# A streaming-encoder trunk: one order of products for each pass, and a longer leash for VectorE

## The chip, the cores and the metric

One core of a Trainium2 chip. The metric is the time of one execution on the device, in microseconds (us). Engines are called as in the profile: PE is TensorE's matmul, PEld its weight load, DVE is VectorE, ACT ScalarE, POOL GpSimd, SP SyncE.

## What is computed

Two pre-norm residual layers over a sequence of 1024 frames and 1024 channels. Each layer projects the normalised input once, runs four token mixers on it, gates and merges them, and projects back:

```python
h = _rmsnorm(x, norm_w)
p = h @ w_in                               # 1024 x (all widths of the four mixers and the gates)
u_a = _rwkv7_branch(...); u_b = _retention_branch(...)
u_c = _ssd_branch(...);   u_d = _gdn_branch(...)
gates = jax.nn.sigmoid(gate_logits.reshape(b, s, N_BRANCH, D_MODEL))
merged = gates[:, :, 0] * (u_a @ w_branch[0]) + ... + gates[:, :, 3] * (u_d @ w_branch[3])
return x + merged @ w_out
```

RWKV-7 and gated DeltaNet (GDN) are recurrences; in chunks they need the inverse of a triangular matrix. A last RMSNorm follows the two layers. All in float32.

## The kernel before, in words

A *pass* is one layer (l) on one half of the frames (512): pass p = 2 l + half, four passes. The weights are cut into *slabs* of 128x512. Each is split into a high and a low part in fp32r (wh, wl), as is the activation (hH, hL), and a product is hH·wh + hL·wh + hH·wl: for one slab 8 matmuls with wh and 4 with wl (`slab_gemm`), into one of three PSUM banks named g. ACT or DVE makes wh (a cast), DVE makes wl by a subtraction in `low`, up to three slabs ahead of use; in the second pass of a layer both come back from DRAM, where SP kept them (ws). SP loads slabs five ahead into three raw buffers (`prefetch`).

A pass is a list of *items*, each with its products. `in.u.role` is an input of unit u: its result goes to one of a few SBUF places (PLACES: in0 to in3 have two, in4 and in5 one), and the item has to wait until a place is free (`unit_input`). `sm` and `lora` are small shared inputs, `merge.kind.i` the gate and the branch projection of a mixer that is through, `gate.i` and `proj.i` those of the last mixer, `norm` the start of the next pass's normalisation, `out.i` a slab of the output projection. The list was written by hand: FIRST for the first pass, PLAN for the other three; in PLAN the `out` items are those of the pass before.

Twelve *units* (UNITS: 2 retention, 4 GDN, 2 SSD, 4 RWKV heads or groups) do the mixers. A unit is a generator (`ret_front`, `gdn_front`, `gdn_mid` with `inverse`, `gdn_back` and so on) that writes a few instructions for all engines at each step and stops where PE would have to wait for another engine. At most two fronts are held at once; backs follow in order.

Nothing is scheduled on the chip: each engine runs its instructions in the order in which Python writes them. `mixers` weaves them. A planner's clock (`Clock`) adds up estimated times for each engine while instructions are written. At each turn `step(LEAD)` looks for a unit step whose inputs are ready by that clock at PE's time; if the clock of DVE is more than LEAD = 3 us beyond PE's, no unit step is written. Where no step is due, the next four or so matmuls of the next item are written (`products`). An item that cannot start yields None; then only unit steps follow until it can, whatever the lag (`step(1e9)`). In this text the product stream *stands* from the first such None to the next matmul of an item.

For the change of a pass: `norm` issues six loads of x on SP and starts `norm_steps`, which writes for each of 8 blocks one multiplication on DVE (`norm_block`), a cast to hH on ACT and a subtraction to hL on DVE (`norm_low`). hH and hL have one buffer each, so they are written after the last gate product of the pass. Until all blocks are written, h counts as not ready (`h_gemm`). Only in the first pass a few items can run early, on rows that are not normalised yet (rH, rL, in the buffers u), with the factor multiplied in afterwards. `proj.i` ends in three DVE instructions with an ACT copy between (`ev` in `proj`). All engine calls but matmuls have line 400 in the profile, matmuls 480, transposes 484.

Of the kernel before, what the change touches and what calls it, by code (L numbers as in the profile page):

```python
# [50 lines left out]
FIRST = items("""
sm in.0.k in.0.q in.0.v in.0.z0 in.0.z1 in.1.k in.1.q in.1.v in.1.z0 in.1.z1 in.2.v in.2.k in.2.q in.2.z in.3.v
in.3.k in.3.q lora in.3.z in.4.v in.4.k in.4.q merge.ret.0 merge.ret.1 merge.ret.2 merge.ret.3 merge.ret.4 in.4.z
in.5.v in.5.k in.5.q merge.ret.5 in.5.z in.6.x0 in.6.B in.6.C in.6.x1 merge.ret.6 merge.ret.7 in.6.z in.7.x0
in.7.B in.7.C in.7.x1 merge.gdn.0 merge.gdn.1 merge.gdn.2 in.7.z in.8.v in.8.k in.8.r in.8.z in.9.v in.9.k in.9.r
in.9.z merge.gdn.3 merge.gdn.4 in.10.v in.10.k in.10.r merge.gdn.5 merge.gdn.6 merge.gdn.7 merge.ssd.0 in.10.z
merge.ssd.1 in.11.v in.11.k in.11.r merge.ssd.2 merge.ssd.3 merge.ssd.4 in.11.z merge.ssd.5 merge.ssd.6
merge.ssd.7 gate.0 gate.1 gate.2 gate.3 gate.4 gate.5 gate.6 gate.7 norm proj.0 proj.1 proj.2 proj.3 proj.4 proj.5  # L60
proj.6 proj.7
""")

PLAN = items("""
in.0.k in.0.q in.0.v in.0.z0 in.0.z1 in.1.k in.1.q in.1.v in.1.z0 out.0 sm out.1 out.2 out.3 out.4 out.5 in.1.z1
in.2.v in.2.k in.2.q in.2.z in.3.v in.3.k in.3.q in.3.z in.4.v in.4.k in.4.q out.6 out.7 lora merge.ret.0
merge.ret.1 merge.ret.2 merge.ret.3 in.4.z in.5.v in.5.k in.5.q merge.ret.4 in.5.z in.6.x0 in.6.B in.6.C in.6.x1
merge.ret.5 merge.ret.6 merge.ret.7 in.6.z in.7.x0 in.7.B in.7.C in.7.x1 merge.gdn.0 merge.gdn.1 in.7.z in.8.v
in.8.k in.8.r in.8.z in.9.v in.9.k in.9.r in.9.z merge.gdn.2 merge.gdn.3 in.10.v in.10.k in.10.r merge.gdn.4
merge.gdn.5 merge.gdn.6 merge.gdn.7 merge.ssd.0 in.10.z merge.ssd.1 in.11.v in.11.k in.11.r merge.ssd.2  # L70
merge.ssd.3 merge.ssd.4 in.11.z merge.ssd.5 merge.ssd.6 merge.ssd.7 gate.0 gate.1 gate.2 gate.3 gate.4 gate.5
gate.6 gate.7 norm proj.0 proj.1 proj.2 proj.3 proj.4 proj.5 proj.6 proj.7
""")
# [38 lines left out]


SLABS = [sl for it in PLAN for sl in slabs_of(it)]
NSLAB = len(SLABS)
SLAB_AT = {sl: n for n, sl in enumerate(SLABS)}


def sequence(npass):

    seq = [(p - (it[0] == "out"), it) for p in range(npass) for it in (PLAN if p else FIRST)]
    return [x for x in seq if x != (npass - 1, ("norm",))] + [(npass - 1, it) for it in PLAN if it[0] == "out"]

# [147 lines left out]
class Clock:  # L271
# [89 lines left out]
    def ported(self, eng, name, ins):  # L361


        if eng == "scalar" or not ins or any(self.slot.get(x.tensor.name, ("",))[0] in ("m", "g", "y") for x in ins):
            return False
        return eng == "gpsimd" or name in ("tensor_tensor", "scalar_tensor_tensor", "tensor_copy", "copy") \
            or (name == "tensor_scalar" and int(np.prod(ins[0].shape[1:])) >= 32)

    def free(self, eng, port=False):
        return max(self.t[eng], self.port) if port else self.t[eng]  # L370
# [2 lines left out]
class Engine:  # L373
# [5 lines left out]
    def __getattr__(self, what):  # L379
        fn = getattr(self.real, what)  # L380

        def call(*a, **k):
            ops = [x for x in list(a) + list(k.values()) if hasattr(x, "ap") and hasattr(x, "tensor")]
            out = k.get("out", a[0] if a else None)
            outs = [out] + ([k["accum_out"]] if k.get("accum_out") is not None else [])
            n = max(int(np.prod(x.shape[1:])) for x in ops)
            if what == "dma_start":
                self.clock.transfer(self.name, a[0], a[1], int(np.prod(a[0].shape)) / 256)
            else:
                nm = "pow" if ALU.pow in a else what  # L390
# [9 lines left out]
            return fn(*a, **k)  # L400
        return call
# [21 lines left out]


class Trunk:
    LEAD = 3.0

    def __init__(self, ctx, tc, io, depth=DEPTH, dbg=None):
        self.tc, self.io, self.depth = tc, io, depth
# [39 lines left out]


    def mm(self, out, lhsT, rhs, **k):
        n, m = (int(np.prod(ap.shape[1:])) for ap in (rhs, lhsT))
        if rhs.dtype != F32:
            cost = max(n, 128) * 0.456e-3
        elif m <= 64:
            cost = 0.03 if m <= 32 else 0.11 if n <= 64 else n * 1.7e-3
        else:
            cost = 2 * max(n, m) * 0.85e-3
        self.ck.op("pe", [out], [lhsT, rhs], cost)
        self.nc.tensor.matmul(out, lhsT, rhs, **k)  # L480
# [6 lines left out]
    def setup(self):  # L487
# [793 lines left out]
    def mixers(self):  # L1281
# [815 lines left out]
```

## Time and profile before

| | us |
|---|---|
| median of 3 runs | 3675.07 |
| lowest and highest | 3674.42, 3675.59 |
| the profiled execution | 3677.53 |
| its span | 3675.8 |
| PE busy in it | 3535.3 |
| DVE, ACT, POOL busy | 2296.0, 1178.1, 572.1 |

The page gives busy time by engine, the granted clock of PE, the chain that ended last and groups of instructions with the idle time before each; "<-" in a row of waits names what ended the wait. A row of a stretch gives start and end in us, its length, then busy us of PE, PEld, DVE, ACT and POOL with counts, the clock granted (1.00 is full), the share of DMA and GB/s. A stretch's length less its PE busy time is called its idle time.

### The profile page before, as it was taken

To read this page: it belongs to the slowest core of one execution; us is meant where nothing else is said; L and a number is where in the kernel's file an instruction comes from. 1 tells how busy PE (TensorE), PEld (TensorE's weight loads), DVE (VectorE), ACT (ScalarE), POOL (GpSimd) and SP (SyncE) were. 2 spreads that over 40 slices of the span, in tenths; PEclk is the share of its full clock that TensorE was granted. 3 is DMA by queue.
4 is the path that set the end of the run, shared out by engine and by line. 5 is a ranking of instruction groups with operands and counts; after the bars stand their busy time and mean duration, and the time that the engine had idled before them with its cause. 6 is when DMAs were issued, how large, how long until landed. Compare 5 with 4: busy or idle time off the path is not lost.

```text
span 3675.8 us, 66687 instructions
## 1 busy us (share of the span) xinstructions
PE 3535.3 (96%) x24904; PEld 2855.0 (78%) x24904; DVE 2296.0 (62%) x6038; ACT 1178.1 (32%) x2714; POOL 572.1 (16%) x905
## 2 busy tenths in 40 slices
PE   8998999999999999999999989999999999999998
PEld 6776887777787888777777777877778788877777
DVE  5676767677356655466547676667764666564653
ACT  4333344333132223232224333433331322232221
POOL 2101012221110111122110101122211011112220
PEclk9998999999999999999999999999999999999999
DMA  6573565656665545444676556655566544544356
GB/s 236 174 232 130 196 211 190 200 165 208 210 211 160 150 133 146 134 111 128 199 252 226 185 187 200 208 185 172 185 215 225 177 152 144 149 132 132 104 153 214
DMA packets 359171, 654.21 MB, mean 178 GB/s; under 512 B 39872, under 2 KB 43328, under 8 KB 358848
## 3 DMA queue, kind: packets, MB, share of 16 engines
q1 hardware_dynamic: 347184, 629.92, 54.3%
q10 hardware_dynamic: 11664, 20.02, 1.6%
q8 instruction: 197, 3.23, 0.4%
q14 instruction: 126, 1.03, 0.1%
HBM read 400.23 MB, written 249.56 MB: 177 GB/s over the span
## 4 chain that ended last, share of the span: by engine, by line
PE 83%; DVE 10%; DMA 2%; ACT 2%; issue 1%; POOL 1%; SPq 0%; DVEq 0%; ACTq 0%; POOLq 0%
PE g L480 60%; PE m L480 17%; PE m L484 3%; PE y L480 3%; DVE invw L400 2%; DVE w L400 1%; DMA ws<-wh 1%; DVE wl L400 1%; DVE in L400 1%; DVE cvy L400 1%; DVE yB L400 1%; POOL rs L400 1%; DVE hL L400 0%; ACT w L400 0%; DVE GD L400 0%
## 5 line engine op out<-in xcount | busy, mean ns | idle before, releaser
L480 PE MATMUL g<-hH,wh 128*128 128x512 f32 x2600 | 1075.8, 414 | 0.0
L480 PE MATMUL g<-hL,wh 128*128 128x512 f32 x2600 | 1034.8, 398 | 16.0 <-DVE hL L400 15.9
L480 PE MATMUL g<-hH,wl 128*128 128x512 f32 x2576 | 745.7, 406 | 0.0
L480 PEld LDWEIGHTS g<-hL,wh 128*128 128x128 f32 x2600 | 492.3, 189 | 128.4 <-DVE hL L400 19.3
L480 PEld LDWEIGHTS g<-hH,wh 128*128 128x128 f32 x2600 | 492.0, 189 | 117.5 <-issue 7.1
L480 PEld LDWEIGHTS g<-hH,wl 128*128 128x128 f32 x2576 | 475.7, 190 | 112.1 <-issue 8.1
L480 PE MATMUL g<-u,wh 128*128 128x512 f32 (+1 forms) x1328 | 409.0, 412 | 18.8 <-DVE u L400 11.8
L400 DVE TENSOR_TENSOR wl<-raw,wh 128x512 fp32r<-128x512 f32 x456 | 331.1, 731 | 61.3 <-ACT wh L400 40.3
L400 ACT CAST wh<-raw 128x512 fp32r<-128x512 f32 x447 | 275.2, 619 | 252.5 <-DMA ws<-wh 106.8
L480 PEld LDWEIGHTS g<-u,wh 128*128 128x128 f32 (+1 forms) x1328 | 245.0, 190 | 81.5 <-DVE u L400 18.0
L400 POOL TENSOR_TENSOR rs<-rs,mhalf 128x4 f32<-128x4 f32 (+2 forms) x80 | 106.1, 1327 | 1011.3 <-DVE rs L400 980.4
L400 DVE SCALAR_TENSOR_TENSOR cvy<-cvraw,par,cvy 128x512 f32<-128x512 f32 x244 | 186.5, 764 | 76.8 <-ACT cvy L400 68.3
L480 PE MATMUL g<-u,wl 128*128 128x512 f32 x784 | 223.4, 403 | 0.0
L400 ACT COPY cvraw<-g 128x512 f32<-128x512 f32 (+1 forms) x160 | 93.5, 584 | 301.5 <-PE g L480 254.3
L480 PEld LDWEIGHTS g<-u,wl 128*128 128x128 f32 x784 | 146.3, 190 | 33.3 <-issue 0.5
L400 ACT ACTIVATE tg<-g 128x512 f32<-128x512 f32 x100 | 59.6, 596 | 267.0 <-PE g L480 258.8
L480 PE MATMUL g<-wh,hL 128*128 128x256 f32 x512 | 126.7, 285 | 6.9 <-DVE hL L400 6.9
L480 PE MATMUL g<-wh,hH 128*128 128x256 f32 x512 | 128.4, 288 | 0.0
L400 POOL TENSOR_SCALAR_AFFINE_SELECT GA<-GA 128x512 f32<-128x512 f32 x128 | 86.5, 681 | 249.8 <-ACT GA L400 215.6
L400 POOL TENSOR_TENSOR acc<-acc,tg 128x512 f32<-128x512 f32 x64 | 84.3, 1317 | 241.9 <-DVE tg L400 176.5
L400 ACT ACTIVATE in<-g 128x512 f32<-128x512 f32 x84 | 49.3, 596 | 187.5 <-PE g L480 182.0
L480 PE MATMUL m<-w,w 64*128 64x256 f32 (+1 forms) x640 | 108.3, 299 | 1.0 <-ACT w L400 1.0
(337 smaller groups left out, 5592.8 us busy)
## 6 DMA issues: line engine op xcount, KB each, us to landing
raw<-W SPq DMA_DIRECT2D x456, 256.0 KB, 3.3
ws<-wh SPq DMA_DIRECT2D x456, 256.0 KB, 3.5
ws<-wl SPq DMA_DIRECT2D x456, 256.0 KB, 3.8
wh<-ws SPq DMA_DIRECT2D x456, 256.0 KB, 2.6
wl<-ws SPq DMA_DIRECT2D x456, 256.0 KB, 3.0
w<-x ACTq DMA_DIRECT2D x32, 256.0 KB, 4.2
tg<-rope SPq DMA_DIRECT2D x16, 256.0 KB, 4.3
cvy<-rope SPq DMA_DIRECT2D x16, 256.0 KB, 4.3
```

The source lines that it names most:

```text
L400: return fn(*a, **k)
L480: self.nc.tensor.matmul(out, lhsT, rhs, **k)
L484: self.nc.tensor.transpose(out, in_, ident)
```

## The change

PLAN and FIRST are replaced by five lists, PLANS: one for each pass, and a last one with the eight `out` items of the last pass. They have the same items in another order. LEAD is 20 instead of 3. The list that numbers the slabs' places in DRAM is now PLANS[1]. `np.prod` in the planner becomes `math.prod`.

```diff
-FIRST = items("""
-sm in.0.k in.0.q in.0.v in.0.z0 in.0.z1 in.1.k in.1.q in.1.v in.1.z0 in.1.z1 in.2.v in.2.k in.2.q in.2.z in.3.v
...
-PLAN = items("""
-in.0.k in.0.q in.0.v in.0.z0 in.0.z1 in.1.k in.1.q in.1.v in.1.z0 out.0 sm out.1 out.2 out.3 out.4 out.5 in.1.z1
...
+PLANS = [items(text) for text in ("""
+in.0.k sm in.0.v in.0.q in.0.z0 in.0.z1 in.1.k in.1.q in.1.v in.2.v in.1.z0 in.2.k in.2.q in.3.v in.3.k lora in.3.q
...
+""", """
+out.0 out.1 out.2 out.3 out.4 out.5 out.6 out.7
+""")]
...
-SLABS = [sl for it in PLAN for sl in slabs_of(it)]
+SLABS = [sl for it in PLANS[1] for sl in slabs_of(it)]
...
-    seq = [(p - (it[0] == "out"), it) for p in range(npass) for it in (PLAN if p else FIRST)]
-    return [x for x in seq if x != (npass - 1, ("norm",))] + [(npass - 1, it) for it in PLAN if it[0] == "out"]
+    return [(p - (it[0] == "out"), it) for p in range(npass + 1) for it in PLANS[p] if (p, it) != (npass - 1, ("norm",))]
...
-    LEAD = 3.0
+    LEAD = 20.0
```

With the new lists the product stream stands 10 times in the whole program, with 104 DVE instructions written meanwhile; with the old ones 27 times, with 404. What that looks like on PE in pass 2, at the third GDN unit's inverse (its 32x32 matmuls, tiles invw and GE) and the second's chain (stgdn is its state, y its output, b its new values). Before, from the end of a stand to its middle:

```order
L484 MATMUL m_22338<-con_81,in_31_20921 128x128 x4
L480 MATMUL m_22365<-GA_19_20982,GR_18_20983 128x128
L480 MATMUL m_22365<-stgdn_1_100,GA_19_20982 128x128
L480 MATMUL y_21934<-stgdn_1_100,GA_19_20982 128x128
L480 MATMUL m_22372<-invw_14_22108,GE_27_22057 32x32 x16
L480 MATMUL m_22391<-b_71_22368,GA_19_20982 128x128
L480 MATMUL y_21934<-b_71_22368,GD_18_20984 128x128
L480 MATMUL m_22395<-invw_14_22108 32x32 x16
L480 MATMUL m_22414<-GA_19_20982,GR_18_20983 128x128
```

After, the same unit on PE (the products are tiles g; lines are 15 further down):

```order
L495 MATMUL g_22148<-hH_19118,wl_22058 128x512 x4
L495 MATMUL g_22148<-hH_19118,wh_22076 128x512
L495 MATMUL g_22148<-hL_19119,wh_22076 128x512
L495 MATMUL g_22148<-hH_19118,wh_22076 128x512
L495 MATMUL g_22148<-hL_19119,wh_22076 128x512
L495 MATMUL m_22183<-invw_14_21985,GE_27_21949 32x32 x16
L495 MATMUL m_22202<-b_71_22129,GA_19_21034 128x128
L495 MATMUL y_21930<-b_71_22129,GD_18_21036 128x128
L495 MATMUL g_22148<-hH_19118,wh_22076 128x512
L495 MATMUL g_22148<-hL_19119,wh_22076 128x512
```

Before, the inverse's first 32x32 matmuls follow the chain's stgdn matmuls at once, and no g product stands among these rows; after, 20 products of 128x512 stand between the stgdn matmuls and these, and more follow.

The second place is DVE at the end of pass 0. w are the loaded blocks of x, hL the low part of the normalised rows, and three rows on in/acc tiles and u are the evacuation of one proj item. Before:

```order
L400 SCALAR_TENSOR_TENSOR in_13_9680<-in_13_9680,g_10014 128x512
L400 TENSOR_TENSOR in_13_9680<-acc_1_2031,in_13_9680 128x512
L400 TENSOR_TENSOR acc_2_10013<-in_13_9680,u_4_9825 128x512
L400 SCALAR_TENSOR_TENSOR w_21_9814<-w_21_9814,par_67,w_17_9792 128x512
L400 TENSOR_TENSOR hL_9808<-w_24_9805,hH_9807 128x512
L400 SCALAR_TENSOR_TENSOR w_25_9820<-w_25_9820,par_67,w_17_9792 128x512
L400 TENSOR_TENSOR hL_9808<-w_21_9814,hH_9807 128x512
L400 TENSOR_TENSOR hL_9808<-w_25_9820,hH_9807 128x512
```

After, from the fourth proj item's evacuation on:

```order
L415 SCALAR_TENSOR_TENSOR in_5_9453<-in_5_9453,g_9916 128x512
L415 TENSOR_TENSOR in_5_9453<-acc_2_2176,in_5_9453 128x512
L415 TENSOR_TENSOR acc_3_9915<-in_5_9453,u_4_9753 128x512
L415 TENSOR_TENSOR hL_9850<-w_25_9877,hH_9849 128x512
L415 TENSOR_TENSOR wl_9962<-raw_9884,wh_9951 128x512
L415 SCALAR_TENSOR_TENSOR in_5_9572<-in_5_9572,g_9947 128x512
```

Before, the last hL row stands behind the evacuation of proj.7; after, behind that of proj.3, with those of proj.4 to proj.7 still to come.

The third place is PE in the first pass, around the input v of unit 0 (128x256 products). Before:

```order
L480 MATMUL m_369<-con_81,yC_272 128x16 x4
L480 MATMUL g_407<-wh_254,hH_274 128x256
L480 MATMUL g_407<-wh_254,hL_275 128x256
L480 MATMUL g_407<-wh_254,hH_274 128x256
L480 MATMUL g_407<-wh_254,hL_275 128x256
```

After:

```order
L495 MATMUL g_228<-u_1_107,wh_173 48x512
L495 MATMUL g_228<-u_1_108,wh_173 48x512
L495 MATMUL g_301<-wh_200,u_1_107 128x256
L495 MATMUL g_301<-wh_200,u_1_108 128x256
L495 MATMUL g_302<-wh_200,u_1_107 128x256
```

Before, these products read the normalised rows hH and hL; after, they read the rows that are not normalised (u_1_107, u_1_108) and follow the 48x512 products of `sm`.

At the end of pass 1, `norm` stands behind gate.7 in both; before, proj.0 to proj.7 follow it, after, proj.7 alone. At the end of pass 0, proj.0 and gate.7 stand before `norm`; at the end of pass 2 the list is as before.

More of the change, by code (lines that the diff above doesn't have):

```diff
@@ L49, in items @@
     return [tuple(int(x) if x.isdigit() else x for x in it.split(".")) for it in text.split()]
-FIRST = items("""
-sm in.0.k in.0.q in.0.v in.0.z0 in.0.z1 in.1.k in.1.q in.1.v in.1.z0 in.1.z1 in.2.v in.2.k in.2.q in.2.z in.3.v
-in.3.k in.3.q lora in.3.z in.4.v in.4.k in.4.q merge.ret.0 merge.ret.1 merge.ret.2 merge.ret.3 merge.ret.4 in.4.z
-in.5.v in.5.k in.5.q merge.ret.5 in.5.z in.6.x0 in.6.B in.6.C in.6.x1 merge.ret.6 merge.ret.7 in.6.z in.7.x0
-in.7.B in.7.C in.7.x1 merge.gdn.0 merge.gdn.1 merge.gdn.2 in.7.z in.8.v in.8.k in.8.r in.8.z in.9.v in.9.k in.9.r
@@ L58 @@
[L58 to L62, printed above, removed]
-PLAN = items("""
-in.0.k in.0.q in.0.v in.0.z0 in.0.z1 in.1.k in.1.q in.1.v in.1.z0 out.0 sm out.1 out.2 out.3 out.4 out.5 in.1.z1
-in.2.v in.2.k in.2.q in.2.z in.3.v in.3.k in.3.q in.3.z in.4.v in.4.k in.4.q out.6 out.7 lora merge.ret.0
@@ L67 @@
[L67 to L71, printed above, removed]
@@ L72 @@
-gate.6 gate.7 norm proj.0 proj.1 proj.2 proj.3 proj.4 proj.5 proj.6 proj.7
-""")
+PLANS = [items(text) for text in ("""
+in.0.k sm in.0.v in.0.q in.0.z0 in.0.z1 in.1.k in.1.q in.1.v in.2.v in.1.z0 in.2.k in.2.q in.3.v in.3.k lora in.3.q
+in.2.z in.1.z1 in.4.k in.3.z in.4.v merge.ret.0 merge.ret.1 in.5.k in.4.q in.5.v merge.ret.2 merge.ret.3 merge.ret.4
+in.4.z in.5.q in.6.x0 merge.ret.5 in.5.z merge.ret.6 in.6.B in.6.C in.6.x1 merge.ret.7 in.7.B in.7.x0 in.6.z in.7.x1
+merge.gdn.0 merge.gdn.1 merge.gdn.2 in.7.C in.8.v in.7.z in.8.k in.8.r in.9.v in.8.z in.9.k merge.gdn.3 in.9.r
@@ new lines @@
+in.9.z merge.gdn.4 merge.gdn.5 merge.gdn.6 merge.gdn.7 in.10.k in.10.r merge.ssd.0 in.10.v in.10.z merge.ssd.1
+in.11.v in.11.k in.11.r merge.ssd.2 merge.ssd.3 merge.ssd.4 in.11.z merge.ssd.5 merge.ssd.6 merge.ssd.7 gate.0
+gate.1 gate.2 gate.3 gate.4 gate.5 gate.6 proj.0 gate.7 norm proj.1 proj.2 proj.3 proj.4 proj.5 proj.6 proj.7
+""", """
+in.0.k in.0.z0 in.0.q out.0 in.0.v in.0.z1 in.1.k in.1.q in.1.v sm out.1 out.2 out.3 out.4 out.5 in.2.v in.1.z0
+in.2.q in.3.v in.2.k in.3.k in.3.q in.2.z out.6 in.1.z1 out.7 in.4.q in.4.k in.4.v lora merge.ret.0 in.3.z
@@ new lines @@
+merge.ret.1 merge.ret.2 in.4.z merge.ret.3 in.5.q in.5.k in.5.v in.5.z in.6.x0 merge.ret.4 in.6.B in.6.C in.6.z
+in.6.x1 merge.ret.5 merge.ret.6 merge.ret.7 in.7.C merge.gdn.0 in.7.x0 in.7.B in.7.x1 merge.gdn.1 in.7.z in.8.v
+in.8.k in.8.z merge.gdn.2 in.9.k in.8.r merge.gdn.3 merge.gdn.4 merge.gdn.5 merge.gdn.6 in.9.v in.9.r in.10.r
+merge.gdn.7 merge.ssd.0 in.9.z in.10.v in.10.k merge.ssd.1 in.11.v in.11.k in.10.z merge.ssd.2 merge.ssd.3 in.11.r
+merge.ssd.4 merge.ssd.5 merge.ssd.6 in.11.z merge.ssd.7 gate.0 gate.1 gate.2 gate.3 gate.4 gate.5 proj.0 gate.6
@@ new lines @@
+proj.1 proj.2 proj.3 proj.4 proj.5 proj.6 gate.7 norm proj.7
+""", """
+in.0.k sm in.0.z0 in.0.q in.0.v in.0.z1 in.1.k in.1.q in.1.v out.0 out.1 out.2 in.2.q out.3 in.2.v in.2.k in.3.v
+in.3.k out.4 in.1.z1 in.1.z0 in.2.z out.5 in.3.q in.3.z in.4.v in.4.k out.6 out.7 lora merge.ret.0 in.4.q
+merge.ret.1 merge.ret.2 merge.ret.3 in.5.q in.4.z in.5.v in.5.k merge.ret.4 in.6.C in.6.B merge.ret.5 in.5.z in.6.x1
+in.6.x0 in.7.B merge.ret.6 merge.ret.7 in.6.z in.7.x0 merge.gdn.0 merge.gdn.1 in.7.x1 in.7.C in.7.z in.8.v in.8.k
@@ new lines @@
+in.8.r merge.gdn.2 in.9.r in.8.z merge.gdn.3 in.9.v in.9.z in.9.k in.10.v in.10.k in.10.r merge.gdn.4 merge.gdn.5
+merge.gdn.6 merge.gdn.7 merge.ssd.0 in.10.z merge.ssd.1 in.11.v in.11.k in.11.r merge.ssd.2 merge.ssd.3 merge.ssd.4
+merge.ssd.5 merge.ssd.6 merge.ssd.7 in.11.z gate.0 gate.1 gate.2 gate.3 gate.4 gate.5 gate.6 gate.7 norm proj.0
+proj.1 proj.2 proj.3 proj.4 proj.5 proj.6 proj.7
+""", """
+in.0.q in.0.z1 in.0.k in.0.v in.0.z0 in.1.q in.1.k in.1.z0 out.0 sm out.1 in.1.v out.2 out.3 in.2.k out.4 out.5
@@ new lines @@
+in.1.z1 in.2.q in.2.v out.6 out.7 in.3.k in.3.q in.2.z in.3.v lora in.3.z merge.ret.0 merge.ret.1 in.4.v merge.ret.2
+in.4.k in.4.q merge.ret.3 in.5.k in.5.q in.4.z in.6.C in.5.v in.6.x0 in.6.B merge.ret.4 in.6.x1 merge.ret.5
+merge.ret.6 in.5.z in.6.z merge.ret.7 in.7.x0 merge.gdn.0 merge.gdn.1 in.7.C in.8.k in.7.x1 in.7.B in.7.z in.8.z
+in.8.v in.8.r in.9.v in.9.k merge.gdn.2 merge.gdn.3 in.9.z in.9.r in.10.v in.10.k in.10.r merge.gdn.4 merge.gdn.5
+merge.gdn.6 merge.gdn.7 merge.ssd.0 in.10.z in.11.v merge.ssd.1 in.11.r merge.ssd.2 merge.ssd.3 merge.ssd.4 in.11.k
@@ L76, in block_cols @@
+in.11.z merge.ssd.5 merge.ssd.6 merge.ssd.7 gate.0 gate.1 gate.2 gate.3 gate.4 gate.5 gate.6 gate.7 norm proj.0
+proj.1 proj.2 proj.3 proj.4 proj.5 proj.6 proj.7
+""", """
+out.0 out.1 out.2 out.3 out.4 out.5 out.6 out.7
+""")]
 def block_cols(kind, idx, role):
@@ L366, in ported @@
         return eng == "gpsimd" or name in ("tensor_tensor", "scalar_tensor_tensor", "tensor_copy", "copy") \
-            or (name == "tensor_scalar" and int(np.prod(ins[0].shape[1:])) >= 32)
+            or (name == "tensor_scalar" and int(math.prod(ins[0].shape[1:])) >= 32)
     def free(self, eng, port=False):
@@ L385, in call @@
             outs = [out] + ([k["accum_out"]] if k.get("accum_out") is not None else [])
-            n = max(int(np.prod(x.shape[1:])) for x in ops)
+            n = max(int(math.prod(x.shape[1:])) for x in ops)
             if what == "dma_start":
-                self.clock.transfer(self.name, a[0], a[1], int(np.prod(a[0].shape)) / 256)
+                self.clock.transfer(self.name, a[0], a[1], int(math.prod(a[0].shape)) / 256)
             else:
@@ L471, in mm @@
     def mm(self, out, lhsT, rhs, **k):
-        n, m = (int(np.prod(ap.shape[1:])) for ap in (rhs, lhsT))
+        n, m = (int(math.prod(ap.shape[1:])) for ap in (rhs, lhsT))
         if rhs.dtype != F32:
```

## The prediction, made before the run

> **What bounds the kernel now.** I read the head of the page first, then the row of cores, then the waits of PE, then stretches of the span by engine, and last the order of time inside the worst stretch.
>
> ```profile
> span 3675.8 us, 66687 instructions
> PE 3535.3 (96%) x24904; PEld 2855.0 (78%) x24904; DVE 2296.0 (62%) x6038; ACT 1178.1 (32%) x2714; POOL 572.1 (16%) x905
> core 0: 3675.8 us, clock 0.981
> ```
>
> PE is the bound: it idles for 3675.8 − 3535.3 = 140.5 us. The second loss is in the clock. A mean grant of 0.981 is (1 − 0.981) × 3675.8 = 69.8 us of full-speed time not granted. A new order removes no product, so only these two sums can shrink.
>
> The rows of PE's waits name VectorE nearly every time:
>
> ```profile
> PE g L480 <- DVE hL L400: 22.8, 6, 7.2
> PE m L484 <- DVE yB L400: 18.8, 9, 4.5
> PE m L480 <- DVE invw L400: 18.7, 19, 4.3
> PE m L480 <- DVE GR L400: 18.2, 5, 6.1
> ```
>
> VectorE is only 62% busy, so the waits are places where PE has been handed nothing but the dependent links of a unit's chain. The kernel's code says when that happens: the next product in PLAN cannot start (its `in` place is taken, or h is not ready), and only unit steps are written until it can. I followed the program in the order in which it is written and marked where the product stream stands. Before, it stands 27 times, and 404 VectorE instructions are written meanwhile. The thirteen stretches of the span that lie on unit inputs (us; length, then PE busy, PEld, DVE, ACT, POOL, then the granted clock):
>
> ```profile
> 103.60:131.00 27.40, 18.76 (x72) 13.19 (x71) 15.26 (x40) 4.87 (x12) 4.18 (x2) 0.77 0.18 63
> 277.50:293.30 15.80, 10.59 (x73) 9.18 (x72) 8.54 (x24) 3.04 (x7) 1.01 (x1) 0.87 0.10 35
> 329.50:354.00 24.50, 14.06 (x146) 11.71 (x145) 16.99 (x62) 3.04 (x8) 2.34 (x6) 0.58 0.17 53
> 403.70:419.20 15.50, 12.85 (x174) 11.30 (x173) 10.82 (x29) 3.03 (x6) 2.71 (x6) 0.89 0.35 105
> ...
> 588.70:597.00 8.30, 5.79 (x90) 5.06 (x90) 6.51 (x27) 2.78 (x7) 3.06 (x5) 0.79 0.54 186
> ...
> 2076.70:2097.10 20.40, 14.76 (x189) 12.85 (x189) 12.45 (x35) 4.23 (x10) 2.15 (x5) 0.86 0.25 86
> 2132.60:2156.00 23.40, 12.02 (x145) 10.02 (x144) 17.01 (x62) 3.04 (x8) 2.34 (x6) 0.71 0.17 57
> ...
> 2289.20:2303.00 13.80, 9.32 (x46) 7.74 (x44) 7.76 (x16) 4.08 (x13) 4.42 (x5) 0.75 0.15 53
> 2392.60:2399.00 6.40, 3.88 (x88) 3.40 (x88) 5.51 (x23) 2.77 (x7) 1.47 (x2) 1.00 0.49 157
> ...
> sum 168.40, PE 111.74 PEld 92.35 DVE 112.34 ACT 37.03 POOL 24.93; mean PE 8.60 PEld 7.10 DVE 8.64 ACT 2.85 POOL 1.92
> ```
>
> They hold 168.40 − 111.74 = 56.7 us of the idle time, and the sum of (1 − clock) × length over the rows with a clock below 1 is 6.3 + 2.1 + 10.3 + 1.7 + 1.7 + 2.9 + 6.8 + 3.5 = 35.2 us, half of the clock's loss. Within the stretch from 2132.6 the rows of PE in order of time show the chain alone:
>
> ```profile
> 2133.44 0.39 PE L480 MATMUL m<-GA,GR 128*128 128x128 f32 x2
> 2136.98 0.49 PE L480 MATMUL m<-stgdn,GA 128*128 128x128 f32 x2 [3.15 <-DVE stgdn L400]
> 2137.31 0.39 PE L480 MATMUL y<-stgdn,GA 128*128 128x128 f32 x2
> 2141.99 0.65 PE L480 MATMUL m<-invw,GE 32*32 32x32 f32 x32 [4.30 <-DVE invw L400]
> ```
>
> The other known losses lie at the first inverse of a pass (190.6, 1104.9, 1993.0, 2916.4), at the first normalisation (37.7) and at the three changes of pass (893, 1804.5, 2704), in the same columns:
>
> ```profile
> 37.70:57.00 19.30, 12.37 (x84) 11.73 (x84) 17.97 (x40) 7.05 (x14) 4.90 (x4) 0.82 0.42 140
> 190.60:207.00 16.40, 10.29 (x44) 7.67 (x43) 13.13 (x40) 5.93 (x11) 0.00 (x0) 0.80 0.58 190
> 893.00:938.00 45.00, 35.65 (x140) 27.39 (x139) 31.28 (x49) 15.06 (x26) 1.68 (x2) 0.92 0.65 219
> 1104.90:1116.00 11.10, 7.76 (x34) 5.72 (x33) 8.66 (x33) 2.41 (x6) 0.00 (x0) 0.85 0.32 94
> 1804.50:1822.00 17.50, 10.25 (x35) 7.89 (x34) 13.67 (x22) 7.98 (x14) 0.81 (x1) 0.80 0.55 170
> 1993.00:2006.00 13.00, 8.77 (x35) 6.46 (x34) 11.02 (x41) 4.10 (x9) 0.52 (x1) 0.74 0.75 248
> 2704.00:2748.00 44.00, 36.27 (x135) 27.91 (x134) 31.26 (x49) 15.06 (x26) 0.90 (x1) 0.84 0.66 223
> 2916.40:2928.00 11.60, 8.26 (x36) 6.21 (x35) 9.48 (x38) 2.42 (x6) 0.00 (x0) 0.85 0.35 94
> ```
>
> Their loss of clock, worked out in the same way, is 3.5 + 3.3 + 3.6 + 1.7 + 3.5 + 3.4 + 7.0 + 1.7 = 27.7 us. Where products are at hand, units cost PE next to nothing, with VectorE busier than its mean:
>
> ```profile
> 2400.00:2500.00 100.00, 99.88 (x841) 78.70 (x840) 66.66 (x184) 35.75 (x78) 22.80 (x40) 1.00 0.58 190
> ```
>
> **The change, part by part.** The PE rate for a product comes from a row of the chain that ended last, 22.86/98 = 0.233 us; VectorE's durations from its groups; the loads' landing from the DMA issues:
>
> ```profile
> 1951.73 22.86 PE g L480 x98
> L400 DVE TENSOR_TENSOR wl<-raw,wh 128x512 fp32r<-128x512 f32 x456 | 331.1, 731 | 61.3 <-ACT wh L400 40.3 <-DMA wl<-ws 13.1 <-DMA ws<-wl 3.9
> L400 DVE TENSOR_TENSOR hL<-w,hH 128x512 fp32r<-128x512 f32 x24 | 16.4, 685 | 0.3
> raw<-W SPq DMA_DIRECT2D x456, 256.0 KB, 3.3
> w<-x SPq DMA_DIRECT2D x16, 256.0 KB, 5.5
> ```
>
> *Stopped stretches.* In the new order the product stream stands 10 times instead of 27, with 104 VectorE instructions instead of 404. One stop is a change of pass, costed below. The rest I price by the nearest row. The two long ones of pass 0 hold 59 instructions between them; the stretch at 329.5 has 62 and idles 24.50 − 14.06 = 10.4 us, so 59/62 × 10.4 = 9.9. Pass 2's stop before in.7.z has 15; the stretch at 2289.2 has 16 and idles 4.5, so 4.2. Those before in.10.v of pass 2 and in.11.v of pass 3 have 5 and 6, like the one at 2392.6, which idles 2.5: 5.0. Three small ones: 1 each. Together 22.1, so 56.7 − 22.1 = 34.6 us go. If idle time went by the count of VectorE instructions alone, 56.7 × 104/404 = 14.6 would stay and 42 go; if the new stretches idle twice as much as the rows, 12 go. I take 34.6, since these rows hold the same kind of steps. The work that covers the chain is products such as the 20 in the order rows above, 4.7 us: they stand where 4.30 us was waited. If a product among them waited itself, that cover would be gone and the wait back.
>
> *First inverse of passes 1 to 3.* It idles 3.3 + 4.2 + 3.3 = 10.9 us. Between the front's VectorE instructions and the first matmul of the inverse lay about 24 PE instructions; now there lie 38 to 74, at least 14 × 0.233 = 3.3 us more. I take all 10.9; half is the other end. Pass 0's lies inside a stop already priced.
>
> *Start.* in.0.k and in.0.v now run on the unnormalised rows, the latter with 96 matmuls while VectorE normalises. The 19.30 − 12.37 = 6.9 us go; the two extra multiplications (0.7 us each) lie beside products. Other end: nothing gained.
>
> *Changes of pass.* After pass 0 the last hL write now stands before four groups of three VectorE instructions. From the norm's start PE has 84 products, 19.6 us, and needs 36 VectorE instructions, 36 × 0.69 = 24.8 us, for the next PSUM bank: it waits 5.2 where it idled 45.00 − 35.65 = 9.35, a gain of 4.1. After pass 2 it is 38 instructions, 26.2, against 96 products, 22.4: 3.8 instead of 7.7, a gain of 3.9. After pass 1 the norm is started later, behind gate.7 and before proj.7 alone. (Before, it was started early, but its last rows stood behind proj.7's evacuation on VectorE:
>
> ```profile
> 1811.53 0.69 DVE L400 TENSOR_TENSOR acc<-in,u 128x512 fp32r<-128x512 f32 x1 [0.68 <-ACT u L400]
> 1812.14 0.74 DVE L400 SCALAR_TENSOR_TENSOR w<-w,par,w 128x512 f32<-128x512 f32 x1
> 1812.80 0.68 DVE L400 TENSOR_TENSOR hL<-w,hH 128x512 fp32r<-128x512 f32 x1
> ```
>
> the first is that evacuation, the others are the norm's.) Its loads are issued about 2 us ahead of PE and land after 5.5; 19 VectorE instructions follow, 13.1; PE has 27 products, 6.3. It waits 3.5 + 13.1 − 6.3 = 10.3 instead of 7.25, a loss of 3.1. The sum is −4.9, with ends −12 and +5.
>
> *LEAD 20 instead of 3.* A unit step is now written although VectorE is up to 20 us behind PE; what it queues on VectorE stands ahead of later wl subtractions and evacuations, and SyncE's loads into raw wait for those subtractions, with wh/wl traffic and the norm's loads behind them. The trace has no lag of that size with products at hand; the row at 2400 bounds it from below at nearly nothing, twice the idle time of the longest stop (10.4) from above at 21. Below nothing it can't be, since what the new LEAD gains is in the count of stops already, which is the new program's. I take +5, near the row at 2400, which has products at hand as the new order has.
>
> *Clock.* Of the 35.2 us in the stops, 34.6/56.7 return, 21.5; the three inverses' 1.7 + 3.4 + 1.7 and the start's 3.5 make 31.8. PE was busy for 111.74/168.40 = 0.66 of such time, the rest is idle time counted already: 21.
>
> The Trainium skill ("TensorE: Matmul & The Clock Gate", Part 1: The HAM clock gate) says that an idle window of about 3.4 us halves the clock. The rows only half agree: of two idle stretches of 2.5 us, at 588.7 and 2392.6, the first saw 0.79 and the second 1.00.
>
> *Sum.* 34.6 + 10.9 + 6.9 + 4.9 − 5 + 21 = 73 us. The profiled execution took 3677.5 (its span and 1.7 around it), 2.4 above the median of 3675.1. 3677.5 − 73 = 3604.5; against the median, **3602**. What costs nothing: the slabs' DMAs move with their items, and SyncE issues as many as before; POOL's additions into acc move with the merges, and POOL is 16% busy; the weights' places in DRAM and the planner's other product function add no instruction. SyncE's cover is the prefetch of five slabs, 60 products or 14 us; without it a load of 3.3 to 5.5 us would show at each slab that is short of it.
>
> **The rivals.** *Half comes back as lag.* VectorE does the same work, and a wait ended by a fuller queue is only moved. For it: pass 0's two stops remain dense. Against: 62% busy, and the row at 2400. Half of the first four terms, 28, less 5, and half of the clock, 10: −33, 3642; with LEAD at its upper end of 21 and no clock back, −7, 3668.
>
> *Slower: wl behind the units.* VectorE runs in order. Its place is the GDN and RWKV units of passes 0 and 2, sixteen in all, where each slab needs a subtraction of 0.73 us, written about three slabs, 36 products or 8.4 us, ahead of use. If LEAD is used up to 20 us there, PE waits 11.6 us each; the gain of 73 is gone at the seventh, and ten give 116 − 73 = +43, 3718. Against: PE's rows quoted above name no wl among the long waits now. The Trainium skill ("Perfetto Trace Analysis", Tensor Engine Instruction) has VectorE as a strict FIFO, which is what this rival needs. The trace agrees: the norm's row at 1812.14 starts only when the evacuation at 1811.53 is through, though PE stands 7.25 us for it.
>
> *The clock returns whole.* The waits that stay are mostly of 1 to 3 us. If none of them halves the clock, all of the 35.2 + 27.7 = 62.9 us return but the 3.5 after pass 1: 59.4 × 0.66 = 39 instead of 21, and the time is 3584. For it speaks the stretch of 2.5 us that kept 1.00, against it the one that fell to 0.79. The 3.4 us window of the Trainium skill would have it so.
>
> *No change.* One wait for another, 3675. That the order is not changed at all is ruled out: nearly every PE row stands elsewhere.
>
> **How the numbers follow.** Forecast (3590 to 3630) 0.52, clock whole 0.13, half back 0.17, slower 0.11, no change 0.07. The range takes the first three with the bounds of the unknown costs: at the low end 42 + 10.9 + 6.9 + 12 of idle time and 39 of clock, 111 us, 3564; at the high end the 3668 of the half that comes back. A measurement of this kernel can tell about 0.2%, 7 us, from no change. Faster 0.52 + 0.13 + 0.17 = 0.82, same 0.07, slower 0.11.
>
> **What would show it.** Right: PE idle near 140.5 − 52 = 88 us, mean clock near 0.99, "m <- DVE invw", "yB" and "GR" together far below 55.7, hL after pass 1 longer than 7.2. Wrong: PE waits "g <- DVE wl" or on evacuations by tens of us (the slower rival), or idle time unchanged under other names.

## The result, and the profile after

The changed kernel takes 3592.29 us (median of 4 runs, 3591.84 to 3592.88); the kernel before, on the same chip, 3675.33 (3674.42 to 3681.01). The ratio is 0.9771, with a 95% interval of 0.9754 to 0.9788: 83 us faster. A second measurement gave 3592.03 against 3675.59.

The head of the page and the row of the core after the change:

```profile
span 3591.1 us, 66655 instructions
PE 3504.1 (98%) x24904; PEld 2832.7 (79%) x24904; DVE 2314.6 (64%) x6044; ACT 1176.7 (33%) x2709; POOL 582.5 (16%) x905
core 0: 3591.1 us, clock 0.989
```

PE has the same 24904 matmuls. The span is 84.7 us shorter. PE's idle time fell from 140.5 to 3591.1 − 3504.1 = 87.0 us, by 53.5; PE's busy time fell by 31.2 us, from 3535.3 to 3504.1. The work is the same, so most of the second sum is the clock: the time not granted fell from 69.8 to 0.011 × 3591.1 = 39.5 us. By the clock's records in the two traces, PE was busy for 98.3 of 142.7 us at half clock before, and for 45.5 of 81.4 us after. Half of the difference, 26.4 us, is an estimate of what working PE got back. What the other 4.8 us are is not shown. An order can move this sum by some us without the clock: the old lists at LEAD 20, below, have the same 3535.3 us of busy PE as the kernel before, at a grant of 0.985 against 0.981.

The waits of PE (total us, times, longest). The lines of the helpers stand 15 further down than before:

```profile
PE m L495 <- DVE invw L415: 17.2, 17, 7.3
PE m L499 <- DVE GA L415: 7.8, 3, 6.8
PE g L495 <- DVE cvraw L415: 7.3, 2, 6.1
PE g L495 <- ACT u L415: 6.6, 1, 6.6
PE g L495 <- DVE cvy L415: 5.2, 2, 5.0
PE g L495 <- DVE hL L415: 5.0, 2, 4.1
PE g L495 <- DVE acc L415: 4.8, 1, 4.8
PE m L499 <- DVE yC L415: 4.6, 1, 4.6
...
PE m L495 <- DVE yB L415: 3.1, 1, 3.1
...
PE m L495 <- DVE GR L415: 1.1, 2, 0.9
...
PE m L499 <- DVE yB L415: 0.3, 1, 0.3
```

Before, invw, yB and GR cost 18.7 + 18.8 + 18.2 = 55.7 us in three rows; the same three now hold 17.2 + 0.3 + 1.1 = 18.6. (yB's row of before is that of the transposes, L484 then and L499 now; the 3.1 us are another wait.) The fall is in yB and GR alone: invw keeps 17.2 of its 18.7 us. hL fell from 22.8 to 5.0. No row of PE's waits names wl. New among the long ones are cvraw and cvy (evacuations, that is, reads of a finished PSUM bank, at changes of pass), acc (an evacuation at the start), yC, and a single long wait on GA. The 6.6 us on ACT's u are the kernel's first wait and were there before.

The stretches in which the new order hands PE only unit links, in the columns used before (start and end, length, then busy time of PE, PEld, DVE, ACT, POOL, then the granted clock):

```profile
164.10:168.60 4.50, 4.24 (x31) 3.73 (x30) 4.23 (x11) 2.23 (x7) 1.80 (x3) 1.00 0.28 73
177.90:199.10 21.20, 5.76 (x107) 4.00 (x106) 14.80 (x46) 3.91 (x9) 5.09 (x7) 0.56 0.24 75
...
2211.20:2221.00 9.80, 5.25 (x30) 4.52 (x29) 7.59 (x15) 2.74 (x6) 1.03 (x2) 0.85 0.50 161
2316.40:2318.30 1.90, 1.90 (x44) 1.64 (x43) 1.17 (x4) 1.69 (x5) 1.59 (x3) 1.00 0.68 144
...
3290.60:3298.60 8.00, 5.41 (x87) 4.68 (x87) 5.59 (x22) 3.48 (x8) 1.85 (x4) 0.67 0.13 41
```

Their idle time is 0.3 + 15.4 + 4.6 + 0 + 2.6 = 22.8 us, where 56.7 lay in thirteen stretches. Two thirds of it is in one place, pass 0's stop before in.3.z. The changes of pass and the start:

```profile
862.00:905.00 43.00, 34.96 (x144) 27.39 (x143) 26.31 (x41) 13.06 (x22) 5.52 (x4) 0.92 0.66 227
1748.00:1768.00 20.00, 14.71 (x47) 10.02 (x46) 15.57 (x26) 8.20 (x15) 0.00 (x0) 0.74 0.71 224
2630.00:2665.00 35.00, 27.60 (x109) 21.07 (x108) 28.10 (x45) 12.70 (x22) 0.08 (x1) 0.95 0.74 259
37.70:57.00 19.30, 14.50 (x61) 11.71 (x60) 16.59 (x42) 7.92 (x16) 2.82 (x3) 0.82 0.84 265
```

They idle 8.0, 5.3 and 7.4 us (before: 9.35, 7.25 and 7.7), and 4.8 at the start (before: 6.9).

### The profile page after: what moved, and what is told of

It is laid out like the page before. It is cut to its first block, busy times and chain, and to the rows that moved or that the text cites. A ratio compares the mean times of both kernels' runs of the same rounds, so it can differ in the third digit from the quotient of the medians.

```text
span 3591.1 us, 66655 instructions
## 1 busy us (share of the span) xinstructions
PE 3504.1 (98%) x24904; PEld 2832.7 (79%) x24904; DVE 2314.6 (64%) x6044; ACT 1176.7 (33%) x2709; POOL 582.5 (16%) x905
## 4 chain that ended last, share of the span: by engine, by line
PE 87%; DVE 8%; DMA 2%; issue 1%; ACT 1%; SPq 0%; POOL 0%; DVEq 0%; ACTq 0%
PE g L495 64%; PE m L495 17%; PE m L499 3%; PE y L495 3%; DVE invw L415 2%; DVE w L415 1%; DVE wl L415 1%; DVE in L415 1%; DVE cvy L415 1%; DMA ws<-wl 0%; SPq L415 0%; DVE yB L415 0%; DVE hL L415 0%; DVE GD L415 0%; DVE GA L415 0%
## 5 line engine op out<-in xcount | busy, mean ns | idle before, releaser
L495 PE MATMUL g<-hH,wh 128*128 128x512 f32 (+1 forms) x2608 | 1078.5, 414 | 5.0 <-DVE acc L415 4.8
L495 PE MATMUL g<-hL,wh 128*128 128x512 f32 (+1 forms) x2608 | 1032.4, 396 | 5.1 <-DVE hL L415 5.0
L495 PEld LDWEIGHTS g<-hH,wh 128*128 128x128 f32 (+1 forms) x2608 | 492.3, 189 | 117.8 <-issue 8.4
L495 PEld LDWEIGHTS g<-hL,wh 128*128 128x128 f32 (+1 forms) x2608 | 492.8, 189 | 109.0 <-DVE hL L415 7.3
L495 PE MATMUL g<-u,wh 128*128 128x512 f32 (+1 forms) x1312 | 396.3, 409 | 24.4 <-DVE cvraw L415 7.3
L415 DVE TENSOR_TENSOR wl<-raw,wh 128x512 fp32r<-128x512 f32 x456 | 331.4, 734 | 52.9 <-ACT wh L415 39.5
L495 PE MATMUL g<-wh,hL 128*128 128x256 f32 x480 | 118.3, 283 | 0.0
```

## The experiments

Four theories were on record. S: the time goes by the number of VectorE instructions written while the product stream stands (404 before, 104 after), whichever part of the change brings it about. O: the order of the lists makes the gain, and LEAD little of it. W: a long LEAD costs waits on wl and on evacuations. L: the lists fit each pass as they are, and an item moved by hand, or one list for several passes, loses time.

### LEAD or the lists

Old lists, LEAD 20:

```diff
-    LEAD = 3.0
+    LEAD = 20.0
```

> The old lists with LEAD 20. Theory S (PE's loss goes with the VectorE instructions written while the product stream stands, whatever made it stand): the stream stands 16 times with 124 such instructions, against 404 before and 104 in the changed kernel; 83 us for 300 of them is 0.277 us each, so 3675 - 280 x 0.277 = 3598. Theory O (the lists carry the gain, LEAD little): 3665 to 3680, as before. Rival W (a lag of up to 20 us makes PE wait for wl and evacuations): above 3685, with PE waits on wl.

Measured: 3663.23 us, ratio 0.9961 [0.9946, 0.9976]. New lists, LEAD 3:

```diff
-    LEAD = 20.0
+    LEAD = 3.0
```

> The new lists with LEAD 3. Theory S: 18 stands with 293 VectorE instructions, so 3675 - 111 x 0.277 = 3644. Theory O: 3590 to 3605, nearly all of the gain. Rival W: below 3592, since the lag is gone.

Measured: 3658.70 us, ratio 0.9947 [0.9930, 0.9963]. So by the ratios the one part gives about 14 us, the other about 19, and both together 84. The change is neither of its parts. O falls with the second kernel, of which it wanted 3590 to 3605; the first lies 2 us below its span. W, which wanted above 3685 and below 3592, falls in both. S, which wanted 3598 of the first and 3644 of the second, falls as a measure. Three stands of the first kernel show why (old lists, LEAD 20, same columns):

```profile
111.70:129.50 17.80, 12.67 (x43) 8.16 (x44) 11.03 (x32) 1.93 (x5) 2.92 (x1) 0.72 0.12 42
...
569.10:583.30 14.20, 9.17 (x164) 7.82 (x164) 8.29 (x32) 4.60 (x12) 4.39 (x8) 0.65 0.36 112
...
2365.10:2379.20 14.10, 9.07 (x164) 7.78 (x164) 8.18 (x32) 4.59 (x12) 4.39 (x8) 0.64 0.37 114
```

They idle 5.1, 5.0 and 5.0 us. The kernel has only 124 VectorE instructions in its stands, but the last two of these hold 9 each by the written order and idle 5 us, twice as long as the stands at the same items before (2.5 us, 6 instructions each). The long leash wrote the early steps of the units sooner, which emptied the stands; what is left in them are the last links, each of which PE waits out. A count of instructions says nothing about that.

W's waits are there all the same. Of the two kernels, only this one (old lists, LEAD 20) waits on wl, and its waits on evacuations are as large:

```profile
PE g L480 <- DVE cvy L400: 9.6, 3, 4.7
PE g L480 <- DVE wl L400: 8.9, 7, 2.2
...
PE g L480 <- DVE cvraw L400: 6.8, 4, 2.2
```

The kernel before has no such rows. What it loses there this kernel gets back elsewhere: its waits on hL are 3.1 us, against 22.8.

In the second kernel (new lists, LEAD 3) the stands come back, 18 with 293 VectorE instructions. The longest is in pass 1, where the changed kernel has none and the kernel before none longer than 2.4 us:

```profile
1239.40:1266.20 26.80, 12.04 (x145) 10.30 (x144) 15.69 (x48) 3.72 (x7) 2.35 (x6) 0.60 0.07 22
```

It idles 14.8 us at a clock of 0.60. In this kernel the wait on invw reaches 37.0 us (longest 11.3) and that on hL 26.1:

```profile
PE m L495 <- DVE invw L415: 37.0, 27, 11.3
PE g L495 <- DVE hL L415: 26.1, 7, 7.6
```

So the new lists put inputs where their places are free only if the units' steps have been written early; with LEAD 3 these steps are held back, the place is taken, and the stream stands in front of it.

### Which pass

New lists in pass 0 alone, then in passes 1 to 3 alone, both with LEAD 20:

```diff
+PLANS = [PLANS[0]] + [OLD_PLAN] * 3 + [PLANS[4]]
```

> LEAD 20, the new list for pass 0, the old one for passes 1 to 3. Theory S: 14 stands with 115 instructions, 3675 - 289 x 0.277 = 3595. Theory O: of the 83 us the part of pass 0, which held 31.4 of the 57.4 us idle in stands, about 40: 3635.

```diff
+PLANS = [OLD_FIRST] + PLANS[1:]
```

> LEAD 20, the old list for pass 0, the new ones for passes 1 to 3. Theory S: 12 stands with 113 instructions, 3675 - 291 x 0.277 = 3594. Theory O: the other part, about 43: 3632.

Measured: 3622.00 us, ratio 0.9852 [0.9837, 0.9866], and 3629.08, ratio 0.9871 [0.9857, 0.9886]. Against the old lists at LEAD 20 (3663.23) that is 41 us for pass 0's list and 34 for the other three; both together, the changed kernel, take 71 off. Once LEAD is 20, the lists nearly add up. S, which gave 3595 and 3594, misses both by 27 to 35 us; O's shares, 3635 and 3632, miss by 13 and 3.

### What the stands are worth

After these four I took another measure: not the instructions in a stand but PE's idle time in it. I followed each program in its written order, as in the prediction, marked the PE instructions at both ends of each stand, and added up PE's idle time between them in that kernel's trace. In us:

| kernel | stands, VectorE instructions | idle in stands | PE idle in all (page) | clock | median |
|---|---|---|---|---|---|
| before | 27, 404 | 57.4 | 140.5 | 0.981 | 3675 |
| new lists, LEAD 3 | 18, 293 | 69.5 | 131.4 | 0.979 | 3659 |
| old lists, LEAD 20 | 16, 124 | 48.1 | 126.4 | 0.985 | 3663 |
| new in passes 1 to 3 | 12, 113 | 34.8 | 102.9 | 0.987 | 3629 |
| new in pass 0 | 14, 115 | 35.6 | 104.3 | 0.984 | 3622 |
| changed | 10, 104 | 24.0 | 87.0 | 0.989 | 3592 |
| one list for 1 to 3 | 10, 89 | 17.0 | 84.6 | 0.991 | 3586 |
| two items moved | 9, 49 | 10.2 | 79.3 | 0.990 | 3586 |
| both of these | 9, 34 | 3.5 | 77.8 | 0.994 | 3578 |

The count puts five kernels of 89 to 124 instructions side by side whose times lie 77 us apart; the idle time in the stands orders them, up to differences under 7 us of it, with one exception. That one is the new lists at LEAD 3: more idle time in stands than before, and still 17 us faster, because outside of the stands it idles 131.4 − 69.5 = 61.9 us where the kernel before idles 140.5 − 57.4 = 83.1. The lists shift work also where no product waits for a place, and for this they don't need LEAD: the waits on GR, nearly all of them at first inverses, were 18.2 us before and are 0.9 in that kernel.

### Going on: two items, and one list

The stop before in.3.z holds two thirds of what is left. In pass 0's list, `lora` goes behind in.1.z1 and in.3.z behind in.4.v:

```diff
-in.2.k in.2.q in.3.v in.3.k lora in.3.q
-in.2.z in.1.z1 in.4.k in.3.z in.4.v merge.ret.0
+in.2.k in.2.q in.3.v in.3.k in.3.q
+in.2.z in.1.z1 lora in.4.k in.4.v in.3.z merge.ret.0
```

> The changed kernel with two moves in pass 0's list: lora stands right before in.4.k, and in.4.v before in.3.z. The stands of pass 0 with 59 VectorE instructions shrink to 4. Theory S: the 6.8 + 7.3 + 0.9 us that PE idles at 184.8 to 195.8 go to about 4, and with them most of the 23.9 us of halved clock around them, 8 to 10 us: 3592 - 11 - 9 = 3572, within 5. Rival L (a list is fitted as a whole, and any move by hand costs elsewhere what it gains here): 3585 to 3605.

Measured: 3586.26 us, ratio 0.9754 [0.9738, 0.9770]: 6 us below the changed kernel, by number inside L's span and 14 above S's. The rows show why S missed. In the changed kernel, PE's own rows show two waits at that stop (start and length in us; in brackets the idle time before and what ended it):

```profile
184.78 1.09 PE L499 MATMUL m<-con,GA 128*128 128x128 f32 x4 [6.83 <-DVE GA L415]
193.22 0.65 PE L495 MATMUL m<-invw,GE 32*32 32x32 f32 x32 [7.34 <-DVE invw L415]
```

The move took the second and left the first, 6.9 us, which now lies outside of a stand: the idle time in stands leaves it out in the last two rows of the table above, and that column falls more there than PE's idle time in all. The waits on invw and GA of the kernel with the moves:

```profile
PE m L495 <- DVE invw L415: 9.3, 16, 2.6
...
PE m L499 <- DVE GA L415: 6.9, 1, 6.9
```

What the first wait is made of, in the changed kernel, on POOL and then on VectorE:

```profile
180.48 2.90 POOL L415 TENSOR_TENSOR rs<-rs,mhalf 128x16 f32<-128x16 f32 x1 [14.58 <-DVE rs L415]
```

```profile
183.41 1.23 DVE L415 TENSOR_TENSOR GA<-GA,rs 128x1024 f32<-128x1024 f32 x1 [3.01 <-POOL rs L415]
...
185.37 2.33 DVE L415 SCALAR_TENSOR_TENSOR cvy<-cvraw,par,cvy 128x512 f32<-128x512 f32 x3
```

A reciprocal root on POOL takes 2.90 us for 16 columns, VectorE idles 3.01 for it, and then multiplies for 1.23 before PE may transpose. That is a chain through three engines, of few instructions. The second wait begins behind it: four instructions of another unit's convolution (three on cvy, and one on in behind a wait for ACT) stand on VectorE ahead of the inverse's steps. The wait on GA is there with the new lists at LEAD 3 too (6.1 us), so the leash isn't its cause; why the planner's clock takes GA for ready at that point stays open.

Pass 2's list for passes 1, 2 and 3:

```diff
+PLANS = [PLANS[0]] + [PLANS[2]] * 3 + [PLANS[4]]
```

> The changed kernel with pass 2's list for passes 1, 2 and 3. Stands hold 89 VectorE instructions against 104. Theory S: 3592 less 15 x 0.14 to 0.28, about 3589, the same within 0.3%: no pass needs a list of its own, only lists without stands. Rival L: half of the 30 us that the three lists gained together at LEAD 20 is lost, 3605 to 3620.

Measured: 3586.20 us, ratio 0.9758 [0.9743, 0.9772]. S's 3589 fits, and L falls: no pass needs a list of its own. Both edits together:

> The two moves of pass 0 together with pass 2's list for passes 1 to 3; stands hold 34 VectorE instructions. Theory S: both add, about 3569. Rival L: 3595 to 3625.

Measured: 3577.88 us, ratio 0.9736 [0.9721, 0.9750], the fastest kernel of this study: 9 us above S's number and 17 below L's span, so neither was right, but the two gains of 6 us each do add, and slightly more. Its page and core row:

```profile
span 3576.0 us, 66636 instructions
PE 3498.2 (98%) x24904; PEld 2827.9 (79%) x24904; DVE 2295.9 (64%) x6042; ACT 1175.7 (33%) x2711; POOL 581.0 (16%) x905
core 0: 3576.0 us, clock 0.994
```

Since these differences are small, the three were run again side by side on one chip:

> The changed kernel as it is, beside the next two on one chip. Both theories: 3592 us (3590 to 3594), ratio 0.977 to the kernel before.

> The changed kernel with the list of pass 2 for all of passes 1 to 3. Theory S (time goes by VectorE's instructions in the stretches without a product; these are 89 against the changed kernel's 104): 3585 to 3589 us, that is below the changed kernel by 3 to 7 us on the same chip. Rival L (each pass needs a list of its own): above 3592 us.

> Two units moved in pass 0's list and pass 2's list for passes 1 to 3. Theory S (34 such instructions): 3575 to 3580 us, below the changed kernel by 12 to 17 us on the same chip. Rival L: no lower than 3585 us.

Measured: 3592.03 us (3589.36 to 3594.37), 3584.88 (3582.55 to 3587.44) and 3581.00 (3576.99 to 3581.80). The order is as before, and the three spans don't overlap: 7 and 11 us below the changed kernel. The last is 1 us above S's span, and 3 above the first measurement of the same kernel. S's spans were set here after these kernels had been measured once, so they say nothing for its count.

### Filling the stands with matmuls that nobody needs

Is it the idle time itself, or the clock that falls behind it? In the kernel before, three 128x256 matmuls whose result isn't used were written into a bank g at each turn at which the stream stands and h is ready (423 more matmuls in all):

```diff
+            if more and r is None and self.h_ready:
+                self.fill_in()
```

> The kernel before, with 423 matmuls of 128x256 more (141 groups of three, into g banks that nobody reads, 0.118 us each at full clock, 50 us of PE work in all) written where the product stream stands and h is ready. The result is the reference's. Theory C (the halved clock after a wait is a cost of its own, 23 to 35 us in the stands): the filler runs in idle time and keeps the clock up; 3675 - 10 to - 25, so 3650 to 3665 with more work. Rival: the clock costs nothing beyond the idle time: 3675 or, where the filler delays the chain, up to 50 us more, 3725.

Measured: 3684.18 us, ratio 1.0023 [1.0014, 1.0032]. This is within the rival's span and above C's. The page, the core row, a stretch that idled 5.6 us at 0.86 before, and one around the stop that idled 11.4 us at 0.71:

```profile
span 3685.6 us, 67502 instructions
PE 3586.5 (97%) x25327; PEld 2902.2 (79%) x25327; DVE 2296.6 (62%) x6038; ACT 1178.0 (32%) x2714; POOL 572.5 (16%) x905
core 0: 3685.6 us, clock 0.988
```

```profile
2076.70:2097.10 20.40, 18.64 (x226) 16.29 (x224) 10.82 (x34) 4.43 (x11) 2.24 (x6) 1.00 0.34 115
2130.00:2160.00 30.00, 25.34 (x219) 20.71 (x218) 21.75 (x77) 5.29 (x12) 2.87 (x7) 0.90 0.32 104
```

The clock held in the first stretch, at 1.00, and rose to 0.988 in the mean; in the second it still fell, where PE still idles 4.7 us. With the stands marked in the written order as above (each up to the next matmul of an item, the unneeded ones not counted as such), PE's idle time in them fell from 57.4 to 26.9 us, and the time at half clock from 142.7 to 90.1 us. PE's busy time rose by 51.2 us all the same, about the 50 us of the matmuls themselves. So here a higher clock was bought with work and saved no time. Theory C's 3650 to 3665 failed, but this run neither shows nor refutes that the halved clock is a cost of its own: what the filler costs by its place in front of the chain's links, and what the clock saves, these figures don't part.

## Why the prediction was right, point by point

The forecast was 3602, the measurement 3592. By its own terms, in us:

| term | forecast | measured |
|---|---|---|
| stopped stretches | −34.6 | 56.7 to 22.8: −33.9 |
| first inverse, passes 1 to 3 | −10.9 | 10.9 to 0: −10.9 |
| start | −6.9 | 6.9 to 4.8: −2.1 |
| changes of pass | −4.9 | 24.3 to 20.7: −3.6 |
| LEAD | +5 | none beyond the rows above |
| first inverse, pass 0 | not counted | 6.1 to 0 outside of stops: −6.1 |
| a new wait in pass 2 | none | +3.1 |
| PE idle, by the page | −52 | −53.5 |
| clock (PE busy) | −21 | −31.2 |

That the idle sum came out within 2 us is luck: two errors of 5 and 6 us on one side (LEAD, pass 0's inverse) met four on the other (start, changes, stops, the new wait) of together 10.

*Stopped stretches.* The sum was right by chance, its parts were not. Pass 0's two stops were priced at 9.9 us by the count of VectorE instructions and idle 15.7; the others were priced at 12.2 and idle 7.1. The experiments show that the count isn't the measure. The count was also not taken alike: the 59 are instructions written in the stands, the 62 those that ran in the stretch, of which 47 were written in its stand, and 59/47 × 10.4 would have been 13.1. The wait on GA, the second longest that is left, contains 3 us for POOL, which no count of VectorE instructions holds.

*First inverse.* Right: the waits of 3.3, 4.2 and 3.3 us on GR are gone. The row quoted above has 1.1 us left in all, 0.9 at the longest. The forecast left pass 0's out ("Pass 0's lies inside a stop already priced"). In the kernel before it lies outside of the thirteen stretches, in the row at 190.6 with 16.40 − 10.29 = 6.1 us, so this gain was missing from the sum. The new wait of the table, 3.1 us on yB in pass 2 (2174.8 to 2177.9), lies in no row of the forecast.

*Start.* Failed. "The 19.30 − 12.37 = 6.9 us go" overlooked what the products on unnormalised rows end in. On VectorE their evacuation (acc, with the factor nrs) stands behind the many small steps of `sm`, and PE waits for the bank:

```profile
45.36 1.91 DVE L415 SCALAR_TENSOR_TENSOR yB<-yB 128x48 f32<-128x48 f32 x8
...
48.45 1.28 DVE L415 TENSOR_TENSOR acc<-g,nrs 128x512 f32<-128x512 f32 x2
```

```profile
49.28 0.76 PE L495 MATMUL g<-hH,wh 128*128 128x512 f32 x1 [4.80 <-DVE acc L415]
```

The forecast has these multiplications "lie beside products"; one of them is now what PE waits for.

*Changes of pass.* The sum is near (3.6 us gone, not 4.9), but each part was off. After pass 0 and pass 2 I counted VectorE instructions against PE's products and forecast 5.2 and 3.8; 8.0 and 7.4 were measured. VectorE's rows after pass 0 show the evacuation standing behind the normalisation's blocks, and PE's row the wait for it:

```profile
868.11 0.68 DVE L415 TENSOR_TENSOR hL<-w,hH 128x512 fp32r<-128x512 f32 x1
868.71 0.68 DVE L415 SCALAR_TENSOR_TENSOR cvraw<-cvraw,g 128x512 f32<-128x512 f32 x1
...
869.54 2.90 PE L495 MATMUL g<-u,wh 128*128 128x512 f32 x6 [6.07 <-DVE cvraw L415]
```

The mechanism was the forecast's, the size was not: the balance for a whole change of pass is no measure for a bank that is needed in the middle of it. After pass 1 the sign was wrong: a loss of 3.1 us was forecast, because the normalisation starts later, and 2.0 were gained; hL is not "longer than 7.2" but 4.1 at the most. Whether the normalisation starts late or early there matters little: the kernel with pass 2's list in passes 1 to 3 starts it early and idles 40.00 − 34.54 = 5.5 us, against 5.3:

```profile
1740.00:1780.00 40.00, 34.54 (x143) 25.79 (x142) 29.95 (x52) 15.35 (x28) 2.56 (x2) 0.96 0.63 210
```

*LEAD.* The forecast put it at +5 of new waits and counted its gain among the stands. No wait came beyond the terms above: PE's waits name no wl, and with these lists the written order at LEAD 40 is word for word that at LEAD 20, so at 20 the leash holds nothing back any more. But at the start and the changes of pass the long leash shows. There cvraw, cvy and acc hold 17.3 us, where the same lists at LEAD 3 have

```profile
PE g L495 <- DVE cvraw L415: 0.3, 1, 0.3
```

and no row for the other two, but 26.1 us on hL against 5.0. These are the waits on evacuations that the forecast named as a sign of the slower rival; they came in exchange for waits on hL. The second part was right, and larger than the text makes of it: without LEAD the lists give 19 us of 84.

*Clock.* The mechanism was right, the term too small: 21 forecast, 31.2 measured. The raw sum was good, 31.8 us of grant to return against 69.8 − 39.5 = 30.3. The term that was mis-sized is "PE was busy for 111.74/168.40 = 0.66 of such time". The share was taken over whole stretches; but the clock falls late in a wait and stays low over the work behind it. Of the 142.7 − 81.4 = 61.3 us at half clock that went, PE was busy in 98.3 − 45.5 = 52.8, a share of 0.86; that makes 26.4 us, and the 4.8 us above it stay open. The wait of 7.25 us of the kernel before, cut where the clock changes:

```profile
1806.30:1811.40 5.10, 0.00 (x0) 0.00 (x0) 3.79 (x6) 1.66 (x3) 0.00 (x0) 1.00 0.75 209
1811.40:1818.20 6.80, 4.66 (x11) 3.69 (x12) 6.58 (x11) 3.45 (x7) 0.00 (x0) 0.50 0.47 153
```

The idle 5.1 us have the full clock, and of the 6.8 us at half PE works for 4.66. What was lost to the clock was lost mostly on work.

*The rivals.* "Half comes back as lag": no; idle time outside of the stands fell as well, from 83.1 to 63.0 us. "Slower: wl behind the units": its place exists, as the old lists at LEAD 20 show, but with 8.9 us in seven waits, the longest 2.2, where 11.6 each was its price; with the new lists it isn't seen. The rule of the Trainium skill that it needs ("Perfetto Trace Analysis", Tensor Engine Instruction: VectorE as a strict FIFO) holds all the same: the evacuation at 868.71 above starts only behind the normalisation's subtraction, though PE, which fills the banks, has stood since 863.5. "The clock returns whole" stood at 39 us; 31.2 came, between it and the forecast, and the measured 3592 is a little nearer to its 3584 than to 3602. Its condition did not hold: 81.4 us at half clock stay, and the clock still fell at waits of 3.1 and 2.6 us (at 2177.2 and 3293.3 us). The largest piece is the one stop of pass 0, where the clock is at half for 23.9 us on end:

```profile
180.40:193.20 12.80, 1.09 (x4) 0.72 (x4) 8.29 (x27) 0.63 (x1) 3.56 (x3) 0.50 0.39 123
193.20:204.30 11.10, 9.82 (x120) 7.48 (x121) 7.37 (x18) 4.20 (x10) 1.53 (x4) 0.50 0.08 14
```

## What to carry to other kernels

An order of work that is written out and the rule that holds work back are one change: measured apart they gave 14 and 19 us, together 84 (by the ratios), so neither can be judged with the other at its old value. Price a stretch without bulk work by its idle time in a trace, link by link through all engines, and not by a count of instructions on one engine. And a long wait can cost twice: its own length, and the low clock over the work behind it. Filling it with work that nobody needs keeps the clock but didn't save time here.

## What the runs showed of the hardware

The granted clock falls within a long wait and returns some time after it: in the rows above, full over the first 5.1 us of idle time and half over the 6.8 us that follow; with two waits of 6.8 and 7.3 us close together, half for 23.9 us. Summed over the clock's records, the kernel before spends 142.7 us at half clock, the changed kernel 81.4, and the fastest kernel 43.3 (53.2 when it ran again).

Matmuls whose result nobody needs keep the clock up: 423 of them raised the mean grant from 0.981 to 0.988 and cut the time at half clock from 142.7 to 90.1 us, in a kernel that grew slower by 0.23%.

POOL's power on 128x16 takes 2.90 us, more than VectorE's multiplication of 128x1024 behind it (1.23 us).
